# A two-layer diffusion step on one core: layer input in three steps, modulation sums three slots in four and on into the output projection

## The chip, the cores and the metric

The kernel runs on one core of a Trainium2 chip. A core has five engines with a queue each: TensorE (PE in the profile) multiplies matrices, VectorE (DVE) and ScalarE (ACT) work element by element, GpSimd (POOL) does the same and issues some DMAs, and SyncE (SP) issues most DMAs. The metric is the device time of one launch in microseconds (us): a median of 2555.88 us in 3 runs (2555.37 to 2557.2).

## The reference

Tokens are 128 of a prompt and 512 of a sample, each a vector of 2048. Two layers are computed. In both, `c` and `c_ctx` give a shift, a scale and a gate for the sample and for the prompt:

```
mod = silu(c) @ w_ada[l] + b_ada[l]         -> shift, scale, gate (2048 each)
h   = rmsnorm(x, norm_pre[l]) * (1 + scale) + shift
o   = mixer(h @ w_in[l]) @ w_out[l]
x   = x + gate * rmsnorm(o, norm_post[l])
```

Layer 0's mixer is windowed attention with a sink beside a neighbourhood attention, both with a SiLU gate; layer 1's is a retention in two directions with a gate. Besides `x`, the keys, values and states are given out. All is float32.

## The kernel before

**Layout.** Tokens lie along the free dimension: 640 columns, first the prompt's 128, then the sample's 512, in two column groups of 384 and 256. The 2048 features are 16 tiles of 128 partitions; `y`, `hi` and `lo` hold all 16.

**Numbers.** A float32 product is made of three matmuls on rounded parts: an operand x is split into hi (x rounded, by ACT) and lo (x - hi, by DVE), and hi*hi, hi*lo and lo*hi are summed.

**Slots.** The weights of the four projections come as 732 pieces of 128x512, a slot each. `load_slot` issues the load (SP, tile `wraw`, 5 buffers), `split_slot` makes `whi` (ACT, L277) and `wlo` (DVE, L278; 4 buffers each), and the main loop issues the slot's matmuls (L1374 and L1315). The split for slot s+4 is put behind slot s. The order is that of the program's text on each engine: an instruction that waits holds all behind it on its engine. The first input projection has 188 slots with both column groups (24 matmuls each), the first output projection 128 slots: 64 with the group of 384 columns, then 64 with that of 256 (12 matmuls each).

**Lanes.** Work beside the matmuls is put into lanes: `chain` (norms, residuals, next layer's input), `rope`, `heads` (attention, retention) and `adal` (modulation sums). `step_all`, called once a slot and where room or an end is waited for, moves each lane on by a step, in that order.

**Modulation sums.** Layer 0's shift and scale come first, by matmuls. The other four vectors (gate of layer 0; shift, scale and gate of layer 1) are 256 units, each a load of 128x512 of `w_ada` (`adaraw`, 4 buffers) and two sums `acc += raw * c`, for prompt and sample. DVE does them (L800), but for 80, where ACT scales the raw tile in place (L797) and POOL adds it (L798). 16 units are a group; at its end the sums are cut into three bfloat16 parts (`adab`), and TensorE sums them over the partitions (L824). A group takes 11 steps, of one or two units or of the cutting; there are 16 groups. The lane is emptied before the first output projection.

**Layer input.** For layer 0, POOL multiplies x by the row of 1/rms (`rbc`, L387), DVE multiplies by the scale and adds the shift (L393, two column parts, as prompt and sample have their own), ACT makes `hi`, DVE `lo`. For layer 1 (`hk`), DVE multiplies by `rbc` (L1002), POOL scales and shifts (L1008, the group of 384 in two parts), ACT makes `hi` (L1012), DVE `lo` (L1015). Layer 1's first group is made while the second half of the first output projection runs, its second group under the first slots of the next projection.

**Border of the layers.** Before the output projection, `y_split` cuts the 16 gated tiles of layer 0 into `hi` and `lo` (L1291, L1292). `evac_out` takes each output tile out of PSUM, squares it, sums the squares on POOL (L886) and issues, at its fifth tile, the first loads of the residuals (`load_x`).

Of the kernel before, what the change touches and what calls it, by code (L numbers as in the profile page):

```python
# [38 lines left out]
KP = 4  # L39
CATCH = (4, 7, 10, 13)  # L40
NORM_AT = 2

# [120 lines left out]
def body(tc, io):  # L163
# [67 lines left out]
    def parts(c0, c1):  # L231

        return [(a, b, v) for a, b, v in ((c0, min(c1, TP), 0), (max(c0, TP), c1, 1)) if a < b]

    def unperm(dst, m0, nm):

        return dst.rearrange("p (r m c) -> p m r c", r=8, m=4)[:, m0:m0 + nm]
# [44 lines left out]
    with ExitStack() as st:  # L282
# [82 lines left out]
        def queue_h(kt):  # L365
            t = {}

            def row():
                t["row"] = r = s1.tile([2, 256], F32, name="adarow", bufs=2)
                nc.vector.tensor_copy(r, rowps[kt][0:2, :256])  # L370
                for j in range(1, 4):
                    nc.vector.tensor_tensor(r, r, rowps[kt][32 * j:32 * j + 2, :256], op=ALU.add)

            def turn():
                for i in range(2):
                    nc.tensor.transpose(rowps[kt][:, 256 + 2 * i:258 + 2 * i], t["row"][:, 128 * i:128 * i + 128],
                                        ident[:2, :2])

            def mods():
                ps = rowps.pop(kt)  # L380
                nc.vector.tensor_scalar(sh[0][:, kt, :], ps[:, 256:258], cols[:, 0, 2, kt:kt + 1], None, op0=ALU.add)
                nc.vector.tensor_scalar(am[0][:, kt, :], ps[:, 258:260], bsc1[:, kt:kt + 1], cols[:, 0, 0, kt:kt + 1],
                                        op0=ALU.add, op1=ALU.mult)
                done.add(("mods", kt))

            def scale_x():
                nc.gpsimd.tensor_tensor(x[:, kt, :], x[:, kt, :], rbc, op=ALU.mult)  # L387
                done.add(("scaled", kt))

            def mod_x():  # L390
                u = x[:, kt, :]
                for a, b, v in parts(0, T):
                    nc.vector.tensor_scalar(u[:, a:b], u[:, a:b], am[0][:, kt, v:v + 1], sh[0][:, kt, v:v + 1],  # L393
                                            op0=ALU.mult, op1=ALU.add)

            def split_x():
                u = x[:, kt, :]
                nc.scalar.activation(hi[:, kt, :], u, AF.Copy)
                nc.vector.tensor_tensor(lo[:, kt, :], u, hi[:, kt, :].bitcast(F32), op=ALU.subtract)
                done.add(("h", kt))  # L400

            h_l.add([row, None, turn, mods], [("row", kt)])
            s_l.add([scale_x], ["rbc"] + ([("mods", kt - 1)] if kt > 1 else []))
            x_l.add([mod_x, split_x], [("mods", kt), ("scaled", kt)])

        def queue_d(q):
            ns, kt, after = FIRST_SEQ[q]
# [33 lines left out]
        x_l, s_l, w_l = Lane(done), Lane(done), Lane(done)  # L441
        for kt in range(KT):
            queue_h(kt)
        for q in range(len(FIRST_SEQ)):
            queue_d(q)
        lanes0 = (d_l, s_l, x_l, w_l, h_l)

        def squares(i):
            for kt in range(4 * i, 4 * i + 4):
# [47 lines left out]

    def step_all():
        for ln in lanes:
            ln.step()  # L500

    def room(tag, n, bufs):
# [14 lines left out]
        return g  # L517


    L0 = ExitStack()  # L520
    at = L0.enter_context(tc.tile_pool(name="at", bufs=1))
    AB = {"st": ExitStack()}
# [256 lines left out]

    def ada_load(i):  # L780
        if i < NADA:
            ada_raw[i] = at.tile([128, 512], F32, name="adaraw", bufs=4)
            nc.sync.dma_start(ada_raw[i], io["ada1"][i])

    accs = {}
# [1 line left out]
    def ada_unit(i, pool=False):  # L787
        kt = i % KT
        r = ada_raw.pop(i)
        if kt == 0:  # L790
            for v in range(2):
                accs[v] = at.tile([128, 512], F32, name="adaacc", bufs=2)
                nc.vector.tensor_scalar(accs[v], r, cvec[:, kt, v:v + 1], None, op0=ALU.mult)
        else:
            for v in range(2):
                if v == 1 and pool:
                    nc.scalar.activation(r, r, AF.Copy, scale=cvec[:, kt, 1:2])  # L797
                    nc.gpsimd.tensor_tensor(accs[1], accs[1], r, op=ALU.add)  # L798
                else:
                    nc.vector.scalar_tensor_tensor(accs[v], r, cvec[:, kt, v:v + 1], accs[v], op0=ALU.mult, op1=ALU.add)  # L800
    parts3 = {}

    def ada_part(i):

        for v in range(2):
            parts3[i, v] = at.tile([128, 512], BF16, name="adab", bufs=4)
# [62 lines left out]

    def evac_out(l, n, pss, gs):  # L870
        c = norm_state(l)
        cp = c["pool"]
        for gi in gs:
            a, b = GROUPS[gi]
            w = b - a
# [35 lines left out]
    def queue_chain(l, gi):  # L911
# [85 lines left out]
        def hk(n):  # L997
            t = {}

            def h1():  # L1000
                t["u"] = cp.tile([128, 384], F32, name="u", bufs=6)
                nc.vector.tensor_tensor(  # L1002
                    t["u"][:, :w], y[:, n, a:b], st["rbc"][:, :w], op=ALU.mult)

            def h2():
                u = t["u"]
                for a2, b2, v in parts(a, b):
# [11 lines left out]
            return [h1, h2, h3, h4]  # L1019

        chain.add([None, n1("acc"), None, n2, flag("rbc")])
        for n in range(0, KT, 2 if last else 1):
# [11 lines left out]
    def open_layer1():  # L1034
        st = ExitStack()
        R["st"] = st
        R["qkv"] = st.enter_context(tc.tile_pool(name="qkv", bufs=1))
        R["norm"] = ExitStack()
        norm_state(0)["pool"] = R["norm"].enter_context(tc.tile_pool(name="nrm0", bufs=1))

    def open_retention():
# [293 lines left out]
    while s < NS:  # L1335
        job, kind, role, gs, unit, half, i, ni, w = slots[s]
        if s == firsts["w_out_even"]:
            drain([rope, heads, adal])
            AB["st"].close()
            L0.close()  # L1340
            open_layer1()
        if s == firsts["w_in_odd"]:
            pass
        if s == firsts["w_out_odd"]:
# [2 lines left out]
            norm1 = ExitStack()  # L1347
            chain.new = 1
            norm_state(1)["pool"] = norm1.enter_context(tc.tile_pool(name="nrm1", bufs=1))
        i0 = KP // 4 if role[0] == "rest" else 0  # L1350
        if i == i0:
            pss = {}
# [34 lines left out]
        if place(s) == 1:  # L1387
            ahead(s)
        if s in (end0, end1):
            drain([rope, heads] + ([adal] if s == end0 else []))  # L1390
        for k in ysplit_at.get(s, ()):
            y_split(k)
        s += 1
# [123 lines left out]
```

## Time and profile before

| | |
|---|---|
| median of 3 runs | 2555.88 us |
| profiled execution | 2555.74 us, span 2553.9 us |
| PE busy | 2466.1 us (97%) |
| PE weight loads busy | 2386.2 us (93%) |
| DVE busy | 1507.5 us (59%) |
| ACT busy | 994.0 us (39%) |
| POOL busy | 485.3 us (19%) |
| mean granted TensorE clock | 0.992 |
| chain that ended last | PE 67%, of it the main matmuls (L1374) 47% |

Busy shares are means over stages with different limits. Matmuls are pipelined, and the time between two starts is shorter than the length shown of one. The first half of the first output projection begins at 995 us, the second at 1130 us, the second input projection at 1251 us.

### The profile page before, as it was taken

What the parts mean: (1) busy time and instruction counts of PE and PEld (TensorE: products, weight loads), DVE (VectorE), ACT (ScalarE), POOL (GpSimd) and SP (SyncE); (2) the same over time, 40 slices, a digit from 0 to 9 for tenths busy, and PEclk for the clock granted to TensorE, in tenths of its full rate; (3) what the DMA queues carried; (4) which work ended last, traced back from release to release, by engine and by line L of the source; (5) the groups of instructions that cost most, each with busy time, mean ns of one, the idle gap of its engine ahead of it and who ended that gap; (6) DMA issues with size and microseconds to landing.
All of it is one profiled execution on the core that took longest, in us unless ns stands there. A gap on an engine that the chain in (4) does not pass through costs nothing.

```text
span 2553.9 us, 45697 instructions
## 1 busy us (share of the span) xinstructions
PE 2466.1 (97%) x17808; PEld 2386.2 (93%) x17808; DVE 1507.5 (59%) x2770; ACT 994.0 (39%) x2108; POOL 485.3 (19%) x525
## 2 busy tenths in 40 slices
PE   4999999999999999998999999999999999999997
PEld 2689898999999999997999999999999999999996
DVE  7568788887777775348663445252525355364364
ACT  2233454543343435444543333232323333254443
POOL 5012221112112110117430101010101011011132
PEclk9999999999999999999999999999999999999998
DMA  9856444445545532445554221212121221215373
GB/s 347 321 173 185 146 141 135 135 134 186 175 153 174 177 126 88 161 134 189 172 162 140 70 80 62 88 59 87 59 89 62 83 73 61 87 56 176 124 236 131
DMA packets 186442, 347.12 MB, mean 136 GB/s; under 512 B 20912, under 2 KB 45872, under 8 KB 185712
## 3 DMA queue, kind: packets, MB, share of 16 engines
q1 hardware_dynamic: 182368, 333.25, 39.7%
q0 software_dynamic: 3712, 10.82, 1.2%
q8 instruction: 139, 2.28, 0.4%
q14 instruction: 79, 0.65, 0.1%
q10 hardware_dynamic: 144, 0.13, 0.0%
HBM read 325.51 MB, written 15.99 MB: 134 GB/s over the span
## 4 chain that ended last, share of the span: by engine, by line
PE 67%; DVE 4%; issue 2%; POOL 2%; DMA 1%; ACT 1%; SPq 0%; DVEq 0%; ACTq 0%; POOLq 0%
PE ps_d L1374 47%; PE ps_d L1315 12%; PE ps_O L1254 2%; POOL u L1008 1%; DVE wlo L278 1%; DVE adaacc L800 1%; PE ps_O L1158 1%; PE ps_S L1158 1%; DMA wraw<-i_wpack 1%; DVE y L970 1%; PE ps_O L749 1%; PE ps_T L1232 1%; PE ps_S L1246 1%; ACT whi L277 0%; DVE y L967 0%
## 5 line engine op out<-in xcount | busy, mean ns | idle before, releaser
L1374 PE MATMUL ps_d<-hi,whi 128*128 128x384 f32 (+1 forms) x3808 | 1000.8, 316 | 3.4 <-ACT whi L277 3.2
L1374 PE MATMUL ps_d<-hi,wlo 128*128 128x384 f32 (+1 forms) x3808 | 977.9, 311 | 15.8 <-DVE wlo L278 15.5
L1374 PE MATMUL ps_d<-lo,whi 128*128 128x384 f32 (+1 forms) x3808 | 973.5, 309 | 0.0
L278 DVE TENSOR_TENSOR wlo<-wraw,whi 128x512 fp32r<-128x512 f32 x732 | 570.8, 783 | 609.0 <-ACT whi L277 601.7
L1374 PEld LDWEIGHTS ps_d<-hi,wlo 128*128 128x128 f32 x3808 | 629.7, 189 | 22.3 <-DVE wlo L278 21.9
L1374 PEld LDWEIGHTS ps_d<-hi,whi 128*128 128x128 f32 x3808 | 634.3, 189 | 15.3 <-ACT whi L277 4.3
L1374 PEld LDWEIGHTS ps_d<-lo,whi 128*128 128x128 f32 x3808 | 629.3, 189 | 0.0
L277 ACT ACTIVATE whi<-wraw 128x512 fp32r<-128x512 f32 x732 | 455.7, 626 | 439.7 <-PE ps_d L1374 222.0
L800 DVE SCALAR_TENSOR_TENSOR adaacc<-adaraw,cvec,adaacc 128x512 f32<-128x512 f32 x400 | 278.0, 746 | 5.8 <-POOL adaacc L798 5.7
L798 POOL TENSOR_TENSOR adaacc<-adaacc,adaraw 128x512 f32<-128x512 f32 x80 | 102.9, 1286 | 687.6 <-ACT adaraw L797 687.6
L1315 PE MATMUL ps_d<-whi,hi 128*128 128x256 f32 x960 | 151.0, 287 | 0.7 <-ACT qT L650 0.7
L1315 PE MATMUL ps_d<-whi,lo 128*128 128x256 f32 x960 | 144.4, 280 | 0.0
L1315 PE MATMUL ps_d<-wlo,hi 128*128 128x256 f32 x960 | 144.4, 280 | 0.0
L797 ACT ACTIVATE adaraw<-adaraw,cvec 128x512 f32<-128x512 f32 x80 | 57.9, 724 | 207.7 <-DVE adaacc L800 144.6
L1315 PEld LDWEIGHTS ps_d<-whi,hi 128*128 128x128 f32 x960 | 128.1, 189 | 4.9 <-issue 1.4
L886 POOL TENSOR_TENSOR acc<-acc,sq 128x384 f32<-128x384 f32 (+1 forms) x56 | 56.1, 1002 | 397.7 <-ACT sq L882 397.4
L1315 PEld LDWEIGHTS ps_d<-whi,lo 128*128 128x128 f32 x960 | 126.6, 188 | 0.0
L1315 PEld LDWEIGHTS ps_d<-wlo,hi 128*128 128x128 f32 x960 | 126.5, 188 | 0.0
L694 ACT ACTIVATE p<-p,small 128x384 f32<-128x384 f32 (+1 forms) x64 | 42.9, 671 | 149.8 <-DVE small L686 149.8
L1150 DVE SCALAR_TENSOR_TENSOR fr<-ps_T,kdec,fr 128x256 fp32r<-128x256 f32 x64 | 31.0, 484 | 95.7 <-ACT fr L1149 95.7
L1266 POOL TENSOR_TENSOR mv<-mv,mhalf 128x1 f32<-128x1 f32 x40 | 22.0, 550 | 299.6 <-DVE mv L1265 289.2
L1218 POOL TENSOR_TENSOR qS<-q,qS 128x256 fp32r<-128x256 f32 x32 | 25.2, 789 | 278.8 <-ACT qS L1217 278.8
(251 smaller groups left out, 2502.2 us busy)
## 6 DMA issues: line engine op xcount, KB each, us to landing
wraw<-i_wpack SPq DMA_DIRECT2D x732, 256.0 KB, 2.8
adaraw<-i_ada SPq DMA_DIRECT2D x256, 256.0 KB, 2.7
sraw<-i_ada SPq DMA_DIRECT2D x64, 512.0 KB, 5.7
y<-i_xTp SPq DMA_DIRECT2D x4, 1280.0 KB, 8.6
wf<-i_wfirst SPq DMA_DIRECT2D x20, 256.0 KB, 5.5
bias<-i_biasB POOLq DMA_DIRECT2D x8, 640.0 KB, 4.7
x_scratch<-y SPq DMA_DIRECT2D x8, 384.0 KB, 3.9
xres<-x_scratch SPq DMA_DIRECT2D x8, 384.0 KB, 6.4
```

The costliest lines, as they stand in the source:

```text
L277: nc.scalar.activation(h, r, AF.Copy)
L278: nc.vector.tensor_tensor(l, r, h.bitcast(F32), op=ALU.subtract)
L694: nc.scalar.activation(p[:, :nk], src, AF.Exp, bias=sm[:, 0:1], accum_out=sm[:, 1:2])
L797: nc.scalar.activation(r, r, AF.Copy, scale=cvec[:, kt, 1:2])
L798: nc.gpsimd.tensor_tensor(accs[1], accs[1], r, op=ALU.add)
L800: nc.vector.scalar_tensor_tensor(accs[v], r, cvec[:, kt, v:v + 1], accs[v], op0=ALU.mult, op1=ALU.add)
L886: nc.gpsimd.tensor_tensor(c["acc", gi], c["acc", gi], sq[:, :w], op=ALU.add)
L1150: nc.vector.scalar_tensor_tensor(t[:, 1, :], ps[:, :256], R["kdec"][:, d, h:h + 1], t[:, 0, :].bitcast(F32), op0=ALU.mult, op1=ALU.subtract)
L1158: mm(ps[:, 256 * d:256 * d + 256], lhsT=k[:, kp, 128 * d:128 * d + 128], rhs=v[:, vp, ch, :], start=(i == 0), stop=(i == 2))
L1254: mm(ab, lhsT=t["q"][:, qp, d, :], rhs=t["S"][d][sp].rearrange("p i e -> p (i e)"), start=(d == 0 and i == 0), stop=(d == 1 and i == 2))
L1315: mm(pss[j][:, o:o + 256], lhsT=xp[:, k, c0:c0 + 128], rhs=wp[:, 256 * kk:256 * kk + 256], start=(i == 0 and kk == 0 and p == 0 and t in ( ...
L1374: mm(pss[gi][:, :b - a], lhsT=wp[:, 128 * kk:128 * kk + 128], rhs=xp[:, k, a:b], start=(k == 4 * i0 and p == 0), stop=(k == KT - 1 and p = ...
```

## The change

1. The layer input loses a step. `mod_scale` multiplies by the scale and by `rbc` in one DVE operation; `mod_split` adds the shift inside ACT's rounding (`hi`) and again inside DVE's subtraction (`lo`). Each is done per column part. POOL takes no part any more.
2. `step_all` leaves `adal` out in every fourth slot, until the first output projection begins; from there each slot takes a step. The lane is no longer emptied before that projection, but when its thirteenth output tile is taken out.
3. The sums' tiles lie in a pool of their own (`adp`), which is closed there; the pool for the layer's norm work opens only then, and the first residual loads are issued at that tile instead of the fifth. The square sums have a pool that is open earlier (`sum0`).

```diff
+ADA_REST = 4
+ADA_END = 12
+    def mod_scale(u, src, rb, l, n, a, b):
+        for a2, b2, v in parts(a, b):
+            nc.vector.scalar_tensor_tensor(u[:, a2 - a:b2 - a], src[:, a2 - a:b2 - a], am[l][:, n, v:v + 1],
+                                           rb[:, a2 - a:b2 - a], op0=ALU.mult, op1=ALU.mult)
+    def mod_split(u, l, n, a, b):
+        for a2, b2, v in parts(a, b):
+            nc.scalar.activation(hi[:, n, a2:b2], u[:, a2 - a:b2 - a], AF.Identity, bias=sh[l][:, n, v:v + 1])
+        for a2, b2, v in parts(a, b):
+            nc.vector.scalar_tensor_tensor(lo[:, n, a2:b2], u[:, a2 - a:b2 - a], sh[l][:, n, v:v + 1],
+                                           hi[:, n, a2:b2].bitcast(F32), op0=ALU.add, op1=ALU.subtract)
...
-            def scale_x():
-                nc.gpsimd.tensor_tensor(x[:, kt, :], x[:, kt, :], rbc, op=ALU.mult)
             def mod_x():
-                u = x[:, kt, :]
-                for a, b, v in parts(0, T):
-                    nc.vector.tensor_scalar(u[:, a:b], u[:, a:b], am[0][:, kt, v:v + 1], sh[0][:, kt, v:v + 1],
-                                            op0=ALU.mult, op1=ALU.add)
+                mod_scale(x[:, kt, :], x[:, kt, :], rbc, 0, kt, 0, T)
             def split_x():
-                nc.scalar.activation(hi[:, kt, :], u, AF.Copy)
-                nc.vector.tensor_tensor(lo[:, kt, :], u, hi[:, kt, :].bitcast(F32), op=ALU.subtract)
+                mod_split(x[:, kt, :], 0, kt, 0, T)
...
     def step_all():
         for ln in lanes:
+            if ln is adal:
+                AD["slot"] += 1
+                if AD["slot"] % ADA_REST == 0 and "out" not in AD:
+                    continue
             ln.step()
...
+    adp = AD["st"].enter_context(tc.tile_pool(name="adp", bufs=1, side="right"))
-            ada_raw[i] = at.tile([128, 512], F32, name="adaraw", bufs=4)
+            ada_raw[i] = adp.tile([128, 512], F32, name="adaraw", bufs=4)
...
-            if n == 4 and gi == 0:
+            if l == 0 and n == ADA_END and gi == 0:
+                open_norm0()
+            if n == (ADA_END, 4)[l] and gi == 0:
                 for i in range((6, 8)[l]):
                     load_x(l, i)
...
             def h1():
-                nc.vector.tensor_tensor(
-                    t["u"][:, :w], y[:, n, a:b], st["rbc"][:, :w], op=ALU.mult)
+                mod_scale(t["u"], y[:, n, a:b], st["rbc"], 1, n, a, b)
             def h2():
-                    nc.gpsimd.tensor_scalar(u[:, a2 - a:b2 - a], u[:, a2 - a:b2 - a], am[1][:, n, v:v + 1],
-                                            sh[1][:, n, v:v + 1], op0=ALU.mult, op1=ALU.add)
-            def h3():
-                nc.scalar.activation(hi[:, n, a:b], t["u"][:, :w], AF.Copy)
-            def h4():
-                nc.vector.tensor_tensor(lo[:, n, a:b], t["u"][:, :w], hi[:, n, a:b].bitcast(F32), op=ALU.subtract)
+                mod_split(t["u"], 1, n, a, b)
...
+    def open_norm0():
+        drain([adal])
+        AD["st"].close()
         norm_state(0)["pool"] = R["norm"].enter_context(tc.tile_pool(name="nrm0", bufs=1))
...
         if s == firsts["w_out_even"]:
-            drain([rope, heads, adal])
+            drain([rope, heads])
+            AD["out"] = True
```

Where the sums go is seen in DVE's order. At the border of the first input and output projection DVE had this before (`lo<-y,hi` are the gated tiles' splits, `wlo` the weight splits, `msq` the first norm):

```order
L1292 TENSOR_TENSOR lo<-y,hi 128x640 x4
L278 TENSOR_TENSOR wlo<-wraw,whi 128x512
L1292 TENSOR_TENSOR lo<-y,hi 128x640 x4
L278 TENSOR_TENSOR wlo<-wraw,whi 128x512
L587 TENSOR_TENSOR y<-y,qT 128x640
L1292 TENSOR_TENSOR lo<-y,hi 128x640 x4
L278 TENSOR_TENSOR wlo<-wraw,whi 128x512 x66
L212 TENSOR_SCALAR msq<-ps_T 128x3
L219 TENSOR_SCALAR rdiag<-ident,rcol 128x128 x3
L278 TENSOR_TENSOR wlo<-wraw,whi 128x512 x3
L967 TENSOR_TENSOR y<-y,rbc 128x384
```

Here 66 weight splits follow each other with nothing between. In the same place DVE has this after (`adaacc` are the sums, `adab` their bfloat16 parts, `gg` the modulation columns):

```order
L1301 TENSOR_TENSOR lo<-y,hi 128x640 x4
L294 TENSOR_TENSOR wlo<-wraw,whi 128x512
L599 TENSOR_TENSOR y<-y,qT 128x640
L826 TENSOR_TENSOR adaacc<-adaacc,adab 128x512 x2
L1301 TENSOR_TENSOR lo<-y,hi 128x640 x4
L294 TENSOR_TENSOR wlo<-wraw,whi 128x512 x2
L840 COPY gg_82<-ps_d 128x8
L822 TENSOR_TENSOR adab<-adaacc,adab 128x512 x2
L805 TENSOR_SCALAR adaacc<-adaraw,cvec 128x512 x2
L812 SCALAR_TENSOR_TENSOR adaacc<-adaraw,cvec,adaacc 128x512
L294 TENSOR_TENSOR wlo<-wraw,whi 128x512
L842 TENSOR_TENSOR gg_82<-gg_82,ps_d 128x8
```

The last groups of sums now stand between the weight splits: three whole groups of 11 steps from here on, and the columns of the last one, behind which 30 splits follow each other. In TensorE's order the last small matmuls on `adab` stand in front of the 36th slot of the output projection.

In the layer-1 input, first column group, DVE had per slot (`u<-y,rbc` the product, `lo<-u,hi` the rest):

```order
L219 TENSOR_SCALAR rdiag<-ident,rcol 128x128 x3
L278 TENSOR_TENSOR wlo<-wraw,whi 128x512 x3
L1002 TENSOR_TENSOR u<-y,rbc 128x384
L278 TENSOR_TENSOR wlo<-wraw,whi 128x512
L1002 TENSOR_TENSOR u<-y,rbc 128x384
L278 TENSOR_TENSOR wlo<-wraw,whi 128x512
L1002 TENSOR_TENSOR u<-y,rbc 128x384
L278 TENSOR_TENSOR wlo<-wraw,whi 128x512
L1015 TENSOR_TENSOR lo<-u,hi 128x384
```

and after, with POOL's products between them gone, it has:

```order
L221 TENSOR_SCALAR rdiag<-ident,rcol 128x128 x3
L294 TENSOR_TENSOR wlo<-wraw,whi 128x512 x3
L240 SCALAR_TENSOR_TENSOR u<-y,am_80,rbc 128x128
L240 SCALAR_TENSOR_TENSOR u<-y,am_80,rbc 128x256
L294 TENSOR_TENSOR wlo<-wraw,whi 128x512
L248 SCALAR_TENSOR_TENSOR lo<-u,sh_78,hi 128x128
L248 SCALAR_TENSOR_TENSOR lo<-u,sh_78,hi 128x256
```

Per slot two operations of 384 columns became four, of 128 and 256 columns.

## Rows read from the trace of the kernel before

**Rows 1.** Busy by stage: length, PE, PEld, DVE, ACT, POOL; clock, DMA share, GB/s.

```profile
0.00:159.00 159.00, 127.07 (x1045) 86.85 (x1046) 97.79 (x188) 42.59 (x79) 37.28 (x25) 0.97 0.82 298
159.00:995.00 836.00, 817.96 (x6062) 794.82 (x6061) 649.92 (x1252) 350.13 (x751) 161.87 (x174) 1.00 0.48 153
995.00:1130.00 135.00, 135.00 (x766) 135.00 (x765) 47.91 (x69) 58.18 (x115) 14.21 (x14) 1.00 0.43 142
1130.00:1251.00 121.00, 105.99 (x804) 100.46 (x803) 91.22 (x129) 63.99 (x131) 74.96 (x70) 0.97 0.54 177
```

**Rows 2.** What TensorE waited for, whole span; waiter, releaser, us in total, times, longest.

```profile
PE ps_d L209 <- DVE spare L453: 24.0, 1, 24.0
PE ps_d L1374 <- DVE wlo L278: 15.5, 24, 2.3
PE ps_S L718 <- DVE qT L574: 10.9, 5, 4.3
PE ps_T L376 <- DVE adarow L372: 4.8, 2, 3.6
PE ps_T L738 <- DVE p L701: 3.8, 5, 1.7
...
PE ps_S L376 <- DVE adarow L372: 3.1, 1, 3.1
```

**Rows 3.** Timeline of DVE from 175 us: start, length, line, operation, idle before.

```profile
175.70 2.07 DVE L800 SCALAR_TENSOR_TENSOR adaacc<-adaraw,cvec,adaacc 128x512 f32<-128x512 f32 x3
179.13 1.38 DVE L278 TENSOR_TENSOR wlo<-wraw,whi 128x512 fp32r<-128x512 f32 x1 [1.36 <-ACT whi L277]
180.42 1.40 DVE L800 SCALAR_TENSOR_TENSOR adaacc<-adaraw,cvec,adaacc 128x512 f32<-128x512 f32 x2
181.75 0.68 DVE L278 TENSOR_TENSOR wlo<-wraw,whi 128x512 fp32r<-128x512 f32 x1
```

**Rows 4.** Timeline of POOL beside rows 3.

```profile
178.66 1.29 POOL L798 TENSOR_TENSOR adaacc<-adaacc,adaraw 128x512 f32<-128x512 f32 x1 [2.77 <-ACT adaraw L797]
```

**Rows 5.** Timeline of DVE from 192 us: end and start of groups.

```profile
192.58 2.73 DVE L800 SCALAR_TENSOR_TENSOR adaacc<-adaraw,cvec,adaacc 128x512 f32<-128x512 f32 x4
...
195.84 1.28 DVE L814 TENSOR_TENSOR adaacc<-adaacc,adab 128x512 f32<-128x512 f32 x2
...
198.57 0.69 DVE L278 TENSOR_TENSOR wlo<-wraw,whi 128x512 fp32r<-128x512 f32 x1 [0.85 <-ACT whi L277]
...
200.12 1.29 DVE L810 TENSOR_TENSOR adab<-adaacc,adab 128x512 bf16<-128x512 f32 x2
...
204.17 1.37 DVE L278 TENSOR_TENSOR wlo<-wraw,whi 128x512 fp32r<-128x512 f32 x1 [1.31 <-ACT whi L277]
```

**Rows 6.** DVE's splits in the first half of the output projection, grouped by line.

```profile
L278 DVE TENSOR_TENSOR wlo<-wraw,whi 128x512 fp32r<-128x512 f32 x64 | 44.1, 692 | 86.0 <-ACT whi L277 85.9
```

**Rows 7.** Timeline of DVE, 995 to 1001 us: end of the input projection.

```profile
995.51 0.82 DVE L587 TENSOR_TENSOR y<-y,qT 128x640 f32<-128x640 f32 x1 [2.02 <-ACT qT L516]
...
999.36 1.89 DVE L278 TENSOR_TENSOR wlo<-wraw,whi 128x512 fp32r<-128x512 f32 x3
```

**Rows 8.** Timeline of POOL, 1207 to 1217 us: the layer-1 input.

```profile
1207.54 8.32 POOL L1008 TENSOR_SCALAR u<-u,am,sh 128x128 f32<-128x128 f32 x8
1215.83 1.03 POOL L886 TENSOR_TENSOR acc<-acc,sq 128x256 f32<-128x256 f32 x1
```

**Rows 9.** Three DVE lines by source line: count, min/median/max ns, shapes.

```profile
L800 DVE SCALAR_TENSOR_TENSOR adaacc<-adaraw,cvec,adaacc x400: 734/743/1769, 162.1 to 935.0; 128x512 f32<-128x512 f32 x134
...
L1002 DVE TENSOR_TENSOR u<-y,rbc x32: 410/546/1095, 1190.4 to 1315.1; 128x384 f32<-128x384 f32 x16, 128x256 f32<-128x256 f32 x16
...
L416 DVE TENSOR_TENSOR wlo<-wf,whi x20: 671/673/2056, 31.5 to 147.6; 128x512 fp32r<-128x512 f32 x20
```

**Rows 10.** TensorE and its granted clock (PEclk) in short stretches.

```profile
1160.00:1170.00 10.00, 7.76 (x48) 7.34 (x48) 10.00 (x10) 4.32 (x10) 8.14 (x7) 0.83 0.68 219
...
1210.00:1220.00 10.00, 7.27 (x49) 6.08 (x48) 7.51 (x12) 5.36 (x12) 10.00 (x12) 1.00 0.35 123
```

More of the change, by code (lines that the diff above doesn't have):

```diff
@@ L384, in mods @@
                 done.add(("mods", kt))
-            def scale_x():
-                nc.gpsimd.tensor_tensor(x[:, kt, :], x[:, kt, :], rbc, op=ALU.mult)
-                done.add(("scaled", kt))
             def mod_x():
-                u = x[:, kt, :]
-                for a, b, v in parts(0, T):
-                    nc.vector.tensor_scalar(u[:, a:b], u[:, a:b], am[0][:, kt, v:v + 1], sh[0][:, kt, v:v + 1],
-                                            op0=ALU.mult, op1=ALU.add)
+                mod_scale(x[:, kt, :], x[:, kt, :], rbc, 0, kt, 0, T)
             def split_x():
-                u = x[:, kt, :]
-                nc.scalar.activation(hi[:, kt, :], u, AF.Copy)
-                nc.vector.tensor_tensor(lo[:, kt, :], u, hi[:, kt, :].bitcast(F32), op=ALU.subtract)
+                mod_split(x[:, kt, :], 0, kt, 0, T)
                 done.add(("h", kt))
             h_l.add([row, None, turn, mods], [("row", kt)])
-            s_l.add([scale_x], ["rbc"] + ([("mods", kt - 1)] if kt > 1 else []))
-            x_l.add([mod_x, split_x], [("mods", kt), ("scaled", kt)])
+            x_l.add([mod_x, split_x], [("mods", kt), "rbc"])
         def queue_d(q):
@@ L439, in queue_d @@
             d_l.add([None] + [first_dense(n) for n in range(4)], [("h", kt), ("wsplit", q)])
-        x_l, s_l, w_l = Lane(done), Lane(done), Lane(done)
+        x_l, w_l = Lane(done), Lane(done)
         for kt in range(KT):
@@ L445, in body @@
             queue_d(q)
-        lanes0 = (d_l, s_l, x_l, w_l, h_l)
+        lanes0 = (d_l, x_l, w_l, h_l)
         def squares(i):
@@ L517, in gate_evac @@
         return g
+    AD = {"st": ExitStack(), "slot": 0}
+    adp = AD["st"].enter_context(tc.tile_pool(name="adp", bufs=1, side="right"))
     L0 = ExitStack()
@@ L791, in ada_unit @@
             for v in range(2):
-                accs[v] = at.tile([128, 512], F32, name="adaacc", bufs=2)
+                accs[v] = adp.tile([128, 512], F32, name="adaacc", bufs=2)
                 nc.vector.tensor_scalar(accs[v], r, cvec[:, kt, v:v + 1], None, op0=ALU.mult)
@@ L805, in ada_part @@
         for v in range(2):
-            parts3[i, v] = at.tile([128, 512], BF16, name="adab", bufs=4)
+            parts3[i, v] = adp.tile([128, 512], BF16, name="adab", bufs=4)
             if i < 2:
@@ L871, in evac_out @@
         c = norm_state(l)
-        cp = c["pool"]
+        cp = c["sums"]
         for gi in gs:
@@ L1001, in h1 @@
                 t["u"] = cp.tile([128, 384], F32, name="u", bufs=6)
-                nc.vector.tensor_tensor(
-                    t["u"][:, :w], y[:, n, a:b], st["rbc"][:, :w], op=ALU.mult)
+                mod_scale(t["u"], y[:, n, a:b], st["rbc"], 1, n, a, b)
             def h2():
-                u = t["u"]
-                for a2, b2, v in parts(a, b):
-                    nc.gpsimd.tensor_scalar(u[:, a2 - a:b2 - a], u[:, a2 - a:b2 - a], am[1][:, n, v:v + 1],
-                                            sh[1][:, n, v:v + 1], op0=ALU.mult, op1=ALU.add)
-            def h3():
-                nc.scalar.activation(hi[:, n, a:b], t["u"][:, :w], AF.Copy)
-            def h4():
-                nc.vector.tensor_tensor(lo[:, n, a:b], t["u"][:, :w], hi[:, n, a:b].bitcast(F32), op=ALU.subtract)
+                mod_split(t["u"], 1, n, a, b)
                 if n == KT - 1:
                     done.add(("h1", gi))
-            return [h1, h2, h3, h4]
+            return [h1, h2]
         chain.add([None, n1("acc"), None, n2, flag("rbc")])
@@ L1038, in open_layer1 @@
         R["norm"] = ExitStack()
+        norm_state(0)["sums"] = R["norm"].enter_context(tc.tile_pool(name="sum0", bufs=1))
+    def open_norm0():
+        drain([adal])
+        AD["st"].close()
         norm_state(0)["pool"] = R["norm"].enter_context(tc.tile_pool(name="nrm0", bufs=1))
@@ L1349, in body @@
             norm_state(1)["pool"] = norm1.enter_context(tc.tile_pool(name="nrm1", bufs=1))
+            norm_state(1)["sums"] = norm_state(1)["pool"]
         i0 = KP // 4 if role[0] == "rest" else 0
@@ L1389, in body @@
         if s in (end0, end1):
-            drain([rope, heads] + ([adal] if s == end0 else []))
+            drain([rope, heads])
         for k in ysplit_at.get(s, ()):
```

## The prediction

> **What bounds the kernel now.** I read the busy times by stage first [rows 1], then the list of what TensorE waited for [rows 2], then the order of instructions on the vector engine (DVE), and last DVE's timeline slot by slot. A slot is one 128x512 piece of weights: one load, one split into two parts (whi on ScalarE (ACT), then wlo on DVE), and the matmuls that use it. In rows 1 the reader is to see that TensorE is the bound in the input projection (159 to 995 us: 818 of 836 us busy) and wholly in the first half of the output projection (995 to 1130 us: 135 of 135), and that it loses time at the start (159 less 127.1 us busy), of which this change can reach little, and in the second half of the output projection (1130 to 1251 us: 106 of 121). Rows 2 say for what: the sum of squares at the start (24.0 us, untouched here), the modulation columns at the start (adarow, 4.8 and 3.1 us), the rotated queries and softmax in the input projection (10.9 and 3.8 us), and the weight splits (15.5 us), nearly all beside the layer-1 input. So the change has at most these waits to win: 7.9 us at the start, 18 us in the input projection, 15 us at the border of the layers.
>
> **The modulation sums: where they go.** The sums come in 16 groups of 16 loads; a group takes 11 steps, one step per slot. Before, the steps end inside the input projection. After, every fourth step rests there, and the DVE order of after has three whole groups and the end of a fourth between the weight splits of the first output projection: 33 slots in a row with ada work, then one slot of rest work. That projection's slots are short. 64 slots take 135 us [rows 1], so 2.11 us each, and DVE has 44.1 us of work for 64 splits there and idles 86.0 us [rows 6].
>
> What a slot costs DVE when ada work stands before its split is in the timeline. In a step that gives one half of a unit to ACT and GpSimd (POOL), DVE runs three sums (2.07 us), ACT then scales the raw tile and only after that makes whi, so DVE idles 1.36 us, and the split takes 1.38 us instead of 0.68 because POOL adds at the same time [rows 3, 4]: from 175.70 to 180.42, 4.7 us. A step with two sums takes 180.42 to 182.43, 2.0 us [rows 3]. A step with four takes 192.58 to 195.84, 3.3 us; the two subtractions and their split 1.9 us; the step that has only ACT work 1.5 us (0.85 of it idle); the group's first step, from 200.12 to 205.54, 5.4 us [rows 5]. A group is 5.4 + 2 x 2.0 + 4 x 4.7 + 2 x 3.3 + 1.9 + 1.5 = 38 us for 11 slots, 3.45 us a slot. In the input projection that hides, since a slot takes TensorE longer than that there (836 us for 188 slots, 4.4 us). In the output projection it does not: 3.45 against 2.11.
>
> When does DVE start on it? Before, DVE is through with the splits of the layer's result at 999.4, and the fourth weight split of the projection ends at 1000.0 [rows 7]. After, DVE has two steps of four sums (2 x 2.65), two subtractions (1.2), part of a pooled step (1.5) and one more split (0.6) in front of the first full group; 2.0 us of idle time there [rows 7] takes some up. That makes 1006.6. Three groups are 114 us: 1120.6; the last two subtractions 1.3 and, as an estimate, 3 us where the evictions of a job stand between ACT's scaling and its whi: 1125. There TensorE has a small matmul on the summed columns, in its queue ahead of the projection's 36th slot, so it can't run on with the four splits that are ready. Before, that slot began at 995 + 35 x 2.11 = 1069. **Loss 56 us.** Bounds: if the waits between ACT and DVE fell away and only busy time counted, a group would be 25 sums at 0.665 (2.73 for four, each starting before the last has ended), 2 first products at some 0.4, 4 subtractions and 11 splits at 0.6 = 26.4 us, and the loss 1006.6 + 79.2 + 1.3 - 1069 = 18 us; with the evictions in front of every whi of a pooled step and POOL's adds behind its square sums, 65. I take 56, since rows 3 and 5 show these waits as they are, in the same order of instructions.
>
> What the rests give back: DVE gets a quarter of the steps less, at 3.45 us a step nearly 0.9 us a slot out of 4.4. Most of TensorE's 18 idle us there, 10.9 and 3.8 of them in two lines, are times when DVE lagged by up to 4.3 us [rows 1, 2]. I take two thirds of the 18: **gain 12 us**, bounds 4 and 18.
>
> The loads move with the sums. DMA was busy 0.43 of the first half of the output projection and 0.48 of the input projection [rows 1], so room is there. The six loads of residuals are issued eight jobs later, at slot 48 instead of 16; their first use is after slot 64, 16 x 2.11 = 34 us on, so I cost them at nothing, and their tiles wait for the ada pool, whose last reader was ten slots earlier. Cover gone, the residual chain would start late by one load.
>
> **The three-step input, layer 1.** Before, POOL does two products per 384 columns, and between 1207.54 and 1216.85 it does eight of them and one square sum, 9.3 us for four slots [rows 8], so 2.33 us a slot over 16 slots; TensorE idles beside it. After, POOL's part is gone, and DVE has per slot two pairs of scalar_tensor_tensor (128 and 256 columns) instead of two tensor_tensor of 384, and the split. The trace has that operation at 512 columns only: 0.743 us [rows 9], 0.665 from one start to the next. A tensor_tensor of 256 columns took 0.41 [rows 9], one of 512 0.68, so about 1.04 ns a column: 0.40 and 0.27 for the new ones, bounded above by 0.40 for both. A slot is 2 x (0.40 + 0.27) + 0.6 = 1.94 us, at most 2.2. **Gain 16 x 0.39 = 6 us**, bounds 2 and 11 (all that TensorE lost next to this part). What is late next is DVE itself. The second group of columns runs under slots of 2.1 us, hidden before and after.
>
> A row and a rule differ on what POOL still does to DVE. While POOL added (178.66 to 179.96), the split beside it took 1.38 us instead of 0.68 [rows 3, 4]; the sums' own operation has a median of 0.743 and a least of 0.734 in 400 [rows 9], so it seldom met POOL. The Trainium skill (SBUF — State Buffer, section "SBUF: two separate sides") says that a VectorE operation with two SBUF inputs and a GpSimd operation that reads SBUF shut each other out for the whole instruction; the new operations have two such inputs. By that rule the one square sum per four slots would each hold up one of them, some 4 us over the 16 slots, and the gain would be 2 us and the whole 4 us later. The rows don't show the operation of this size next to POOL; the sum keeps 6.
>
> **The three-step input, layer 0.** POOL's 16 products (31 to 60 us) go. DVE trades a product at 128 and 512 columns and a subtraction of 640 for four scalar_tensor_tensor: by the sizes above 2 x (0.67 + 0.27) = 1.9 us, where the uncontended old ones were some 1.2. But next to POOL the first splits took up to 2.06 us for 0.67 [rows 9], which delays adarow, for which TensorE waits 7.9 us [rows 2]. DMA is at 0.82 over the stage [rows 1] and takes part of the rest. **Gain 4 us**, bounds 0 and 8.
>
> **Sum.** The profiled run took 2555.74 us (span 2553.9, and 1.8 around it); the median is 2555.88, so the profile stands for it. 2555.7 + 56 - 12 - 6 - 4 = **2590 us**, 1.3% slower. Its own range, from the terms' bounds taken half way, is 2574 to 2604.
>
> **Rivals.**
> Busy time alone counts: ACT runs ahead of DVE, the waits of rows 3 and 5 don't come back; loss 18, 2555.7 + 18 - 22 = 2552. For it: ACT is idle enough. Against: ACT's scaling overwrites the tile that DVE has just read, so the order forces the wait. 8%.
> The sums hide wholly in the output projection: its 86 us of DVE idle time [rows 6] take them, the three other terms stay: 2534, faster. It decides if a slot with sums costs DVE less than 2.11 us. Against: 2.4 us a slot even by busy time, and only four of the eleven steps are under 2.11. 7%.
> The matmul clock falls. At 1160 to 1170 us TensorE was idle 2.2 of 10 us and the granted clock was 0.83, at 1210 to 1220 idle 2.7 of 10 and the clock 1.00 [rows 10]: the lower level (1.2 GHz) may come with such gaps or not. With TensorE at 2.11 of 3.45 us, the gaps are larger. A mean of 0.83 is hidden (2.5 us a slot under 3.45); at the lower level throughout a slot would take 4.2 us, 35 x 0.77 = 27 us more. Half way: 2604 to 2617, say 2612. 10%. The Trainium skill (TensorE: Matmul & The Clock Gate, section "HAM oscillation — how this bites in real kernels") has it that waits between groups of matmuls bring the lower clock back each time, which is this rival.
>
> **How the numbers follow.** Forecast 75%, the three rivals 8, 7 and 10%. A measurement of this kernel can't tell less than 0.2% (5 us) from no change. Slower: the forecast and the clock, 84% with a little off for their tails; the first rival is near the lower edge of no change and is shared, 5% same; faster 11%. The range 2560 to 2612 leaves out the two rivals below it and half of the clock's.
>
> **What would show it.** Right: the stage from 995 us on, up to the first norm, some 56 us longer, DVE idle there on whi and its splits 3.4 us apart for 33 slots; TensorE waiting there on wlo and, before the column matmuls, on adab; L718's wait under 5 us; no POOL product beside the layer-1 input and splits near 1.9 us apart. Wrong: if that stage stays near 135 us, the second rival holds and the kernel is faster; if its idle time on whi is gone but the splits still lag, the first.

## The result and the profile after

The changed kernel takes 2579.97 us (median of 4 runs, 2579.88 to 2580.83); the kernel before takes 2555.62 us (4 runs) beside it. The ratio is 1.0094, 95% interval 1.0078 to 1.011: slower by 24 us where 34 were forecast. The profiled run's span is 2578.2 us, against 2553.9.

The same stages as in [rows 1], each cut at the matmul with which it really begins (view of busy time by stretch; columns as there):

```profile
0.00:152.93 152.93, 125.36 (x1044) 86.40 (x1045) 93.04 (x204) 48.69 (x95) 8.05 (x9) 1.00 0.83 310
152.93:962.01 809.08, 807.40 (x5964) 788.84 (x5963) 573.43 (x1132) 333.76 (x718) 143.81 (x159) 1.00 0.44 142
962.01:1159.10 197.09, 161.12 (x866) 152.68 (x865) 128.12 (x190) 75.87 (x147) 33.90 (x29) 0.88 0.50 162
1159.10:1275.68 116.58, 101.60 (x805) 97.25 (x805) 94.43 (x161) 70.49 (x147) 41.70 (x38) 1.00 0.57 184
```

Cut in the same way, the kernel before has 158.87, 835.70, 135.67 and 121.22 us there, and 1302.4 after it (1302.5 in the changed kernel). So the start won 5.9 us, the input projection 26.6 and the second half of the output projection 4.6; its first half lost 61.4. The sum is +24.3. Nothing after the border of the layers moved.

What TensorE waited for in that first half (columns as in [rows 2]):

```profile
PE ps_d L836 <- ACT adab L820: 16.8, 8, 4.6
PE ps_d L1385 <- DVE wlo L294: 6.7, 10, 0.8
PE ps_d L836 <- DVE gg L840: 5.6, 1, 5.6
PE ps_d L1385 <- ACT whi L293: 5.2, 5, 1.3
PE ps_d L836 <- DVE adab L822: 1.7, 5, 0.4
```

That is 36.0 us of idle time, and two thirds of it (24.1 us) stand in front of the small matmuls on the summed columns, not in front of the projection's own. The other 25.4 us are busy time: 96 column matmuls (5.3 us in the view by line), and some 20 us in which the same matmuls ran longer, the granted clock being 0.88 over the stage (1.00 before).

One step there with a sum on ACT and POOL, and the next one up to its sums (timeline of DVE, ACT and POOL: start, length, line, operation, idle before):

```profile
1028.14 2.06 DVE L812 SCALAR_TENSOR_TENSOR adaacc<-adaraw,cvec,adaacc 128x512 f32<-128x512 f32 x3
...
1030.24 0.73 ACT L809 ACTIVATE adaraw<-adaraw,cvec 128x512 f32<-128x512 f32 x1 [3.42 <-DVE adaacc L812]
1030.87 0.47 ACT L894 ACTIVATE sq<-ps_d 128x384 f32<-128x384 f32 x1
1031.04 1.30 POOL L810 TENSOR_TENSOR adaacc<-adaacc,adaraw 128x512 f32<-128x512 f32 x1 [3.37 <-ACT adaraw L809]
1031.24 0.73 ACT L900 ACTIVATE y<-ps_d,gg 128x128 f32<-128x128 f32 x2
1031.85 0.64 ACT L293 ACTIVATE whi<-wraw 128x512 fp32r<-128x512 f32 x1
1032.30 1.00 POOL L898 TENSOR_TENSOR acc<-acc,sq 128x384 f32<-128x384 f32 x1
1032.52 1.33 DVE L294 TENSOR_TENSOR wlo<-wraw,whi 128x512 fp32r<-128x512 f32 x1 [2.31 <-ACT whi L293]
...
1033.77 2.07 DVE L812 SCALAR_TENSOR_TENSOR adaacc<-adaraw,cvec,adaacc 128x512 f32<-128x512 f32 x3
```

The reader is to see [rows 3] come back, now where TensorE needs only 2.1 us a slot: ACT's scale waits for DVE's sums (3.42 us idle), whi stands behind it, here behind an eviction too, so DVE idles 2.31 us in place of 1.36; then the split takes 1.33 us beside POOL instead of 0.68. From 1028.14 to 1033.77 the step cost 5.6 us.

DVE's copies of the summed columns mark the groups (timeline of DVE):

```profile
976.09 0.15 DVE L840 COPY gg<-ps_d 128x8 f32<-128x8 f32 x1
...
1016.03 0.16 DVE L840 COPY gg<-ps_d 128x8 f32<-128x8 f32 x1
...
1055.43 0.16 DVE L840 COPY gg<-ps_d 128x8 f32<-128x8 f32 x1
...
1095.79 0.16 DVE L840 COPY gg<-ps_d 128x8 f32<-128x8 f32 x1
```

39.9, 39.4 and 40.4 us for 11 slots (forecast 38, with 3 us for evictions over the three).

Beside the layer-1 input, in place of [rows 8] (timeline of POOL and DVE; `acc<-acc,sq` is a square sum):

```profile
1224.75 0.90 POOL L898 TENSOR_TENSOR acc<-acc,sq 128x256 f32<-128x256 f32 x1 [6.18 <-ACT sq L894]
1224.97 1.23 DVE L240 SCALAR_TENSOR_TENSOR u<-y,am,rbc 128x128 f32<-128x128 f32 x2
1226.12 0.68 DVE L294 TENSOR_TENSOR wlo<-wraw,whi 128x512 fp32r<-128x512 f32 x1
1226.72 0.74 DVE L248 SCALAR_TENSOR_TENSOR lo<-u,sh,hi 128x128 fp32r<-128x128 f32 x2
1227.38 0.73 DVE L240 SCALAR_TENSOR_TENSOR u<-y,am,rbc 128x128 f32<-128x128 f32 x2
1228.04 0.68 DVE L294 TENSOR_TENSOR wlo<-wraw,whi 128x512 fp32r<-128x512 f32 x1
...
1234.28 0.68 DVE L294 TENSOR_TENSOR wlo<-wraw,whi 128x512 fp32r<-128x512 f32 x1
```

DVE runs without a gap, and its splits stand 1.92 us apart (1226.12, 1228.04); every fourth slot has one pair, beside a square sum, stretched from 0.73 to 1.23 us. Four slots take 8.16 us (1226.12 to 1234.28), so 2.04 a slot in place of 2.33 before; over 16 slots that is the 4.6 us won.

### The profile page after: what moved, and what is told of

It reads as the page before. It is cut to its first block, busy times and chain, and to the rows that moved or that the text cites. A ratio compares the mean times of both kernels' runs of the same rounds, so it can differ in the third digit from the quotient of the medians.

```text
span 2578.2 us, 45662 instructions
## 1 busy us (share of the span) xinstructions
PE 2475.0 (96%) x17808; PEld 2393.7 (93%) x17808; DVE 1509.2 (59%) x2818; ACT 1009.8 (39%) x2140; POOL 408.0 (16%) x461
## 4 chain that ended last, share of the span: by engine, by line
PE 52%; DVE 4%; issue 1%; DMA 1%; ACT 0%; POOL 0%; SPq 0%; DVEq 0%; ACTq 0%
PE ps_d L1385 37%; PE ps_d L1324 9%; PE ps_O L1263 2%; DVE wlo L294 1%; PE ps_O L1167 1%; PE ps_S L1167 1%; DMA wraw<-i_wpack 1%; PE ps_T L1241 1%; DVE y L984 1%; PE ps_S L1255 1%; DVE u L240 0%; DVE y L981 0%; PE ps_T L1154 0%; PE ps_T L1281 0%; DVE y L964 0%
## 5 line engine op out<-in xcount | busy, mean ns | idle before, releaser
L1248 ACT ACTIVATE sS<-sT 128x128 fp32r<-128x128 f32 x40 | 12.4, 311 | 147.9 <-DVE sT L1247 147.9
```

## The experiments

Twelve kernels, each timed in five rounds beside the kernel before. Stages in us, each from one profiled run, cut as above; "input" and "output" are the projections of the first layer.

| kernel | time | start | input | output, 1st half | 2nd half | rest |
|---|---|---|---|---|---|---|
| before | 2555.6 | 158.9 | 835.7 | 135.7 | 121.2 | 1302.4 |
| changed | 2580.0 | 152.9 | 809.1 | 197.1 | 116.6 | 1302.5 |
| e1 no rests | 2546.1 | 154.1 | 836.7 | 135.7 | 116.6 | 1301.4 |
| e2 four steps | 2591.7 | 159.8 | 809.2 | 197.1 | 121.9 | 1301.9 |
| e3 no offload in the output projection | 2559.6 | 153.1 | 809.2 | 177.0 | 117.0 | 1302.0 |
| e4 own buffer | 2560.4 | 153.9 | 806.1 | 179.9 | 116.6 | 1302.3 |
| e5 rest 1 in 16 | 2548.6 | 152.9 | 838.1 | 137.3 | 116.4 | 1301.8 |
| e6 rest 1 in 8 | 2563.5 | 153.1 | 832.2 | 154.6 | 116.8 | 1302.8 |
| e7 steps in 2 of 3 slots | 2535.9 | 153.2 | 809.2 | 153.0 | 116.4 | 1303.8 |
| e8 rest 1 in 8, every 2nd slot | 2546.2 | 153.7 | 828.0 | 144.5 | 116.6 | 1301.9 |
| e9 as e7, no offload at all | 2530.9 | 153.0 | 806.1 | 151.1 | 116.6 | 1301.7 |
| e10 rest 1 in 5, every 2nd slot | 2539.6 | 154.4 | 813.0 | 151.0 | 116.5 | 1302.4 |
| e11 idle additions | 2595.9 | 152.9 | 809.2 | 212.2 | 116.6 | 1302.4 |
| e12 no rests, no offload | 2519.6 | 153.6 | 809.2 | 135.7 | 116.6 | 1301.8 |

"Offload" is the sum that ACT and POOL do for DVE. In the first expectations the border of the input projection was read 2.3 us late: 811.4 and 194.8 there are the 809.1 and 197.1 of the table.

**e1, e2: which part does what.**

```
e1: -ADA_REST = 4                e2: scale_x, mod_x, split_x and
    +ADA_REST = 10 ** 6              h1 to h4 as in the kernel before
```

> The changed kernel with one number other: the sums take a step in every slot (no rests), so by the count of the slots (188 for 177 steps) they end in the input projection again, while the three-step input and the pools of their own stay. Theory (what is lost is the 33 steps that run in the first output projection, what is won in the input projection comes from rests and from steps moved out): the first half of the output projection takes 135 to 138 us as before (194.8 in the changed kernel), the input projection is back near 836 us (811.4), and the start's 5.9 and the junction's 4.6 us stay won: 2543 to 2548. Rival (what is won in the input projection comes from the new pools or the three-step input, not from rests): the input projection stays near 811 and the time is about 2521. Second rival (the loss is the pools' and the late opening's, not the steps'): the output projection stays long, and the time is above 2575.

> The changed kernel with the four-step input of before in both layers (a GpSimd product in each), the sums as changed. Theory (the three steps alone win at the start and at the junction): the start is 158.9 us again (152.9), the second half of the output projection 121 (116.6), and the time 2590 (+10.5). Rival (the start and the junction are won because the sums are elsewhere, or because of the pools): the two stages stay as in the changed kernel and the time is 2580 within 3.

Both came out as the theory had it: 2546.1 (ratio 0.996, 0.9946 to 0.9974) and 2591.7 (1.0137, 1.0123 to 1.0151). The loss is the steps in the output projection; the start and the border are the three-step input's, which by itself is worth 10 to 12 us; what the input projection won goes with the rests and the steps that they move out, which e1 does not part.

**e3, e4: why a step costs so much.**

```
e3: -                if v == 1 and pool:
    +                if v == 1 and pool and "out" not in AD:
e4: -                    nc.scalar.activation(r, r, AF.Copy, scale=cvec[:, kt, 1:2])
    +                    rs = adp.tile([128, 512], F32, name="adas", bufs=1)
    +                    nc.scalar.activation(rs, r, AF.Copy, scale=cvec[:, kt, 1:2])
```

> The changed kernel, but from the first output projection on both sums of each unit run on VectorE: ScalarE and GpSimd take no part. Theory (half of the loss is VectorE waiting for a whi that stands on ScalarE behind a scale which waits for VectorE's own sum; 28.3 us of idle there in the changed kernel's trace): some 20 of the 28.3 us go, 15 more sums of 0.69 us come (10.3 us), and the time falls by about 10, to 2566 to 2574. Rival (VectorE's busy time alone sets the pace): 10 us more, about 2590.

> The changed kernel, but ScalarE's scale writes its product to a buffer of its own in place of the block that VectorE still reads, so it need not wait for VectorE's sum of that block; work and order are the same. Theory (as in e3: the wait of ScalarE's scale for VectorE holds up the next whi): the 28.3 us of VectorE's idle time fall under 8, the first half of the output projection gets 18 to 25 us shorter, and the time is 2555 to 2562. Rival (the wait is for something else, or busy time alone sets the pace): 2580 within 3.

2559.55 (ratio 1.0011, 1.0002 to 1.002) and 2560.39 (1.0014, 1.0005 to 1.0023), both 20 us under the changed kernel. e4, which takes out the wait of ACT's scale for DVE and nothing else, shortens the first half of the output projection by 17.2 us (18 to 25 expected); its other 3 us came in the input projection (809.1 to 806.1), where its edit holds too. So at least 17 us of the loss were that wait. e3, which takes out the wait and POOL's adds, shortens the stage by 20.1. DVE's idle time on whi up to the last column matmuls, 28.3 us in the changed kernel, was 4.3 us in e3 and 5.2 in e4. e3 won twice what was expected, with 15 more sums on DVE. That e4, with 15 sums fewer, is no better than e3 was not foreseen. Its timeline (DVE and POOL):

```profile
1014.21 2.07 DVE L813 SCALAR_TENSOR_TENSOR adaacc<-adaraw,cvec,adaacc 128x512 f32<-128x512 f32 x3
...
1015.76 2.27 POOL L811 TENSOR_TENSOR adaacc<-adaacc,adas 128x512 f32<-128x512 f32 x1 [3.29 <-DVE adaacc L813]
...
1016.80 3.10 DVE L813 SCALAR_TENSOR_TENSOR adaacc<-adaraw,cvec,adaacc 128x512 f32<-128x512 f32 x3
```

Three sums that stand nearly alone take 2.07 us, three in the time of the add 3.10; the add takes 2.27 in place of 1.30. DVE was busy 133.9 us in that stage, more than with all sums its own (130.8 in e3) and than in the changed kernel (128.1).

**e11: is that contention?** Adds that nobody waits for, on top of e3:

```
+                    for _ in range(3):
+                        nc.gpsimd.tensor_tensor(AD["scr"][0], AD["scr"][0], AD["scr"][0], op=ALU.add)
```

> The kernel in which VectorE does all sums from the first output projection on (2559.6), with 45 additions of GpSimd added that nobody needs or waits for: three 128x512 sums on a scratch tile in each step in which GpSimd had its part (58 us of GpSimd at 1.29 us). Theory (GpSimd's sums and VectorE's sums of two SBUF inputs hinder one another: in the kernel with its own buffer VectorE's took 1.03 us beside a GpSimd add in place of 0.69 and the GpSimd add 2.27 in place of 1.29): VectorE's work there gets 20 to 45 us longer and the time is 2575 to 2605. Rival (no such contention; that kernel's stretched rows come from its data arriving late): 2558 to 2562.

2595.93 (1.0155, 1.0141 to 1.0169), 36 us over e3; the stage is 35 us longer, and DVE was busy 166.7 us in it in place of 130.8, so the whole of it is DVE's work getting longer. The timeline shows both engines at work, and no operation of one waits for the other:

```profile
1021.18 12.08 POOL L814 TENSOR_TENSOR scr<-scr 128x512 f32<-128x512 f32 x9
1021.25 1.52 DVE L294 TENSOR_TENSOR wlo<-wraw,whi 128x512 fp32r<-128x512 f32 x1 [1.61 <-ACT whi L293]
...
1022.77 2.89 DVE L829 TENSOR_TENSOR adab<-adaacc,adab 128x512 bf16<-128x512 f32 x2
...
1025.58 2.44 DVE L805 TENSOR_SCALAR adaacc<-adaraw,cvec 128x512 f32<-128x512 f32 x2
1027.94 2.97 DVE L819 SCALAR_TENSOR_TENSOR adaacc<-adaraw,cvec,adaacc 128x512 f32<-128x512 f32 x2
1030.84 1.52 DVE L294 TENSOR_TENSOR wlo<-wraw,whi 128x512 fp32r<-128x512 f32 x1
...
1034.39 0.68 DVE L294 TENSOR_TENSOR wlo<-wraw,whi 128x512 fp32r<-128x512 f32 x1
```

While POOL adds, a split takes 1.52 us; after it 0.68.

**e5, e6, e8, e10: how many rests, how many steps.** e5 and e6 change `ADA_REST` alone, to 16 and 8; e8 and e10 set it to 8 and 5, leave the steps of the output projection to DVE alone as e3 does, and let them run in every second slot (`% 2` where e7 below has `% 3`; e10 with `ADA_END = 14`).

> The changed kernel with one rest in 16 slots in place of one in 4: by the count of slots (188 for 177 steps) one or two steps are left for the first output projection. Theory (a step moved out costs 61.4/36 = 1.7 us there and brings 26.6/36 = 0.7 us in the input projection, of which 10 us are TensorE's own work and halved clock, and the rest are waits that the rests relieve): 2546 as without rests, less up to 5 for the rests: 2540 to 2547. Rival (rests themselves, not the steps moved out, win the 26.6 us in the input projection, and few are enough): 2525 to 2535.

> The changed kernel with one rest in 8 slots: some 12 to 13 steps are left for the first output projection. Theory (cost and gain go by the steps moved): 2546 + 13 x 1.7 - 13 x 0.7 = 2559, or with more of the gain from the rests (half of 26.6 us) 2554: 2550 to 2562. Rival (the entry into the output projection, the last columns and the late opening, costs once, whatever the number of steps): 2575 or more.

> As the kernel with one rest in 8, but the 12 to 13 steps left run without ScalarE and GpSimd and in every second slot of the first output projection. Theory (VectorE then has some 6.8 us of work in four slots' 8.4 us, so only the entry and one or two waits for columns remain): the stage is 3 to 9 us over the 135.7 of before, the time 2534 to 2546. Rival (the steps' price stays): within 4 of the kernel with one rest in 8.

> One rest in 5 slots in the input projection, and the steps left (some 27) in every second slot of the first output projection, VectorE alone, end at the 14th column block. Theory (in the input projection the gain goes with the rests, 26.6 us at one in 4 and some 6 at one in 8; in the output projection 8.9 us were lost with every second slot and 13 steps, 17.3 with two of three and 36): some 18 us won, 12 lost: 2536 to 2544, not better than two of three. Rival (one in 5 relieves the heads' waits as one in 4 does): 2528 to 2534, better than two of three.

2548.55 (0.9971, 0.996 to 0.9983), just above the 2540 to 2547 expected; 2563.5 (1.0029, 1.0018 to 1.0039), above 2550 to 2562; 2546.17 (0.9962, 0.9948 to 0.9975), just above 2534 to 2546; 2539.58 (0.9934, 0.9921 to 0.9946), as expected. All four rivals failed, but so did the theory that the gain goes by the steps moved: in the input projection one rest in 16 or 8 gives -1.5 and 4.4 to 8.7 us against e1, one in 5 gives 23.7 and one in 4 27.6. The 4.4 and 8.7 are e6 and e8, which are the same there, so a stage in which TensorE waits is known to some 4 us. Why the gain is not proportional was not found.

**e7, e9: thinner steps, then no offload.**

```
e7: -                if AD["slot"] % ADA_REST == 0 and "out" not in AD:
    +                if AD["slot"] % (3 if "out" in AD else ADA_REST) == 0:
    -ADA_END = 12
    +ADA_END = 14
    with the edit of e3; e9: the same, and "if False:" in e3's place
```

> The kernel without ScalarE and GpSimd in the sums from the first output projection on (2559.6), and in that projection a step only in two of three slots, with the end moved from the 12th to the 14th column block so that 36 steps fit. Theory (VectorE's busy time sets the pace: 11 steps with their 11 splits are some 33 us of it; with 5.5 more splits of 0.68 us it is 36.7 us for 16.5 slots, which TensorE works in 34.9): the stage costs 10 to 20 us over the 135.7 of before in place of 41, and the time is 2530 to 2542. Rival (each step costs its price wherever it stands, since TensorE's columns wait for the newest step): 2557 to 2562.

> The kernel with steps in two of three slots (2535.9), and now no sum on ScalarE and GpSimd in the input projection either: 65 scales and 65 GpSimd adds go there, 65 sums of 0.75 us come to VectorE (49 us in 809). Theory (beside a GpSimd add VectorE's two-input work slows down, and its splits wait for the scales, so handing a sum to GpSimd saves VectorE little): 2533 to 2539. Rival (in the input projection the offload pays, since VectorE has the heads' work there too): TensorE's waits for qT and p come back, and the time is 2541 to 2550.

e7: 2535.93 (0.9921, 0.9907 to 0.9935), as expected; the stage costs 17.3 us over before. e9: 2530.94 (0.9902, 0.9889 to 0.9916), 5 us better, below the range expected. Of that, 3.1 us came in the input projection (809.2 to 806.1): handing sums to POOL had cost time there too.

**e12: no rests and no offload.**

```
-ADA_REST = 4
+ADA_REST = 10 ** 6
-                if v == 1 and pool:
+                if False:
```

> The kernel without rests (2546.1, all sums in the input projection), with no sum on ScalarE and GpSimd: 80 scales and 80 GpSimd adds go, 80 sums of 0.75 us (60 us) come to VectorE. Theory (from the run in which this won 3 us with rests: handing a sum to GpSimd saves VectorE little, since both slow each other down and ScalarE's scales hold up the next whi): 2541 to 2547. Rival (without rests VectorE has no room for them: 650 us of busy time in 837 become 710, and TensorE waits longer for qT): 2550 to 2565.

2519.61 us (0.9857, 0.9841 to 0.9874): 36 us faster than before, 60 faster than the changed kernel, and far below both expectations. The input projection as a whole, first of e1, then of e12 (stretch; columns as above):

```profile
154.11:990.77 836.66, 819.22 (x6061) 796.54 (x6059) 649.77 (x1252) 349.93 (x749) 162.15 (x174) 0.99 0.49 153
```

```profile
153.56:962.74 809.18, 809.18 (x6060) 791.10 (x6059) 650.95 (x1332) 304.64 (x669) 58.77 (x93) 1.00 0.50 158
```

DVE does 80 instructions more in the same busy time, and TensorE never waits; in e1 it waited for the rotated queries (10.2 us) and the softmax (3.8), both made by DVE. Where the time of the 80 sums came from stands in DVE's lines (grouped by line: busy, mean ns, idle before), e1 and then e12:

```profile
L812 DVE SCALAR_TENSOR_TENSOR adaacc<-adaraw,cvec,adaacc 128x512 f32<-128x512 f32 x400 | 277.9, 745 | 5.7 <-POOL adaacc L810 5.6
L294 DVE TENSOR_TENSOR wlo<-wraw,whi 128x512 fp32r<-128x512 f32 x188 | 178.4, 950 | 143.4 <-ACT whi L293 143.1
```

```profile
L812 DVE SCALAR_TENSOR_TENSOR adaacc<-adaraw,cvec,adaacc 128x512 f32<-128x512 f32 x480 | 330.6, 747 | 1.2 <-DMA adaraw<-i_ada 1.2
L294 DVE TENSOR_TENSOR wlo<-wraw,whi 128x512 fp32r<-128x512 f32 x188 | 130.7, 695 | 74.6 <-ACT whi L293 72.8 <-DMA wraw<-i_wpack 1.5
```

The sums cost 52.7 us more, the splits 47.7 us less, since none stands beside an add any more; and DVE's idle time before whi falls by 70 us. Which of the two, the stretched splits or the wait for whi behind ACT's scale, made TensorE wait in the input projection was not separated. Nor was the removal of the offload tried without the three-step input.

## Why the prediction was right, point by point

The direction and the mechanism held: the steps in the output projection lose more than the rest wins, at the pace of DVE's work and its wait for whi. The terms were off like this.

| term | forecast | bounds | measured | shown by |
|---|---|---|---|---|
| steps in the output projection | +56 | 18 to 65 | +61.4 | e1: 135.7 without them |
| rests in the input projection | -12 | -4 to -18 | -26.6 | e1: 836.7 without rests and moved steps |
| three steps, layer 1 | -6 | -2 to -11 | -4.6 | e2: 121.9 without them |
| three steps, layer 0 | -4 | 0 to -8 | -5.9 | e2: 159.8 without them |

**The step that failed** is "What the rests give back", outside its own bounds. It took two thirds of TensorE's 18 idle us as all there was to win. The idle time did fall, by more than that, from 18.0 to 1.7 us (835.70 less 817.66 before; 809.08 less 807.40 after), 16.4 us. Another 10.3 us came from busy time, which the step left out. The column matmuls that moved out with the steps are little of it: e12 has all of them in this stage, waits nowhere and is busy 809.2 us, 1.8 more than the changed kernel and 8.5 less than the kernel before. So some 8.5 us of busy time went with the waits. Matmuls at the lower level of the clock are a part: the granted clock was 0.98 from 200 to 300 and from 400 to 500 us before, in both stretches with a wait for qT (3.6 and 4.3 us), and 1.00 after; by these figures that is, as an estimate, 4 us. The rest has no cause shown.

The prediction's own range, 2574 to 2604, is not what its bounds give half way: with 37 to 60.5 for the steps and -29.5 to -14 for the three gains they give 2563 to 2602. The measured 2580 lies in both.

**The loss** was put together rightly: pooled steps with their wait for whi, 33 slots in a row, the end at the 36th slot. The groups took 40 us in place of 38, and the first began 14.1 us into the stage (976.09) in place of 11.6; DVE has no idle time in between, where the prediction took off 2.0 us for it. The 36th slot began at 1097.55, 135.5 us into the stage, where 130 were forecast. TensorE's waits came the other way round: mostly in front of the column matmuls (24.1 us), which the prediction put second, and 11.9 on wlo and whi. Behind that slot the others are 2.12 us apart again.

**The three steps** came out as worked out: beside the layer-1 input DVE's splits are 1.92 us apart for 1.94, and in layer 0 TensorE's wait for adarow fell from 7.9 to 3.6 us; the other 1.6 us there were busy time.

**Rival one** (busy time alone counts) put the price too low even where its condition is met: with ACT's scale out of DVE's way the stage cost 44 us (e4) and 41 (e3) over before, not 18. e4 has the rival's own 25 sums a group, and a group took 34 to 35 us there, 32 to 34 of them busy, in place of 26.4: DVE's work gets longer beside POOL. In e3 five more sums a group make 29.7 by the rival's figures, and a group took 32 to 34. **Rival two** was wrong for steps in every slot, but in e7 the same work, in two slots of three and on DVE alone, cost 17. **Rival three**, the clock: the granted clock did fall, to 0.84 and 0.80 from 1000 to 1100 us, at some 20 us of longer busy time. The trace speaks for most of it being hidden. Up to the last column matmuls DVE waited only for ACT's whi, and ACT for DVE, but for 0.3 us (20 us of ACT's idle time have no releaser in the profile). The chain that ended last has no TensorE work from 1071.9 to 1092.9, and then (start, length, what):

```profile
1092.88 0.35 PE ps_d L836 x7
1093.22 3.98 PE ps_d L1385 x12
1097.21 0.48 PE ps_d L836 x16
1097.68 61.58 PE ps_d L1385 x348
```

The slot between the last two sets of column matmuls (L836) took 4.0 us in place of 2.1; that much came on top. What came on top before 1071.9 the chain does not show, and no run changed the clock alone. e3, e4 and e7 shorten DVE's work and get the clock back with it (0.92, 0.91, 0.97 over the stage).

**The rule on the shared port** bears out more than the prediction gave it. The Trainium skill (SBUF — State Buffer, section "SBUF: two separate sides") has a GpSimd operation that reads SBUF and a VectorE operation with two SBUF inputs shut each other out. At the border the stretched pair in every fourth slot is that: 0.5 us each, 2 us over 16 slots, half of the rule's 4, and the gain was 4.6, not 6. In e11 the trace agrees in kind: DVE's operations take twice their time. It doesn't show a full lock: in the 12.08 us of nine adds (the shortest of that line took 1.04 us, so 9.4 at least) DVE did eight 128x512 operations that take 4.9 us without POOL, and 14.3 do not fit into 12.08 one after the other.

## What to carry to other kernels

An operation handed to another engine is worth only what the first engine gets back: here a sum of 0.67 us moved from DVE to ACT and POOL cost a split 0.65 us beside the add, and a wait of ACT's queue on top, so undoing it in 80 places won 27 us. Before work is spilled into the next stage, look at what makes it slow where it stands; and where it must be spilled, work that costs the pacing engine more than a slot belongs in two slots of three, not in every one. When waits leave a stage, count the busy time that goes with them too: here 8.5 us beside 18 of idle time.

## What was not expected of the hardware

A DVE operation with one tensor input was stretched by POOL as well: two products of a tile with a column (TENSOR_SCALAR, L805) took 2.44 us beside the adds of e11 and 0.88 without. And the offload's price did not show in the line of the sums (0.745 and 0.747 us a sum in e1 and e12), but in the neighbour that came after: the split's mean of 950 ns, with a median of 692, was the sign of it in the view by line.
